# A one-core decoder layer in fp32r halves: gate of the first column split, place of the state update, grouping of the sample's cached values

## The chip, the core and the metric

The kernel runs on one core of one Trainium2 chip. The core has TensorE (PE) for matrix products, VectorE (DVE) and ScalarE (ACT) for elementwise work, GpSimd (POOL) for a smaller share of it, and SyncE (SP), whose queue issues the transfers (DMA). The metric is the time on the device of one launch, in microseconds (us), as the median of several runs. Lower is better.

## The reference

One layer of a hybrid decoder is computed for two groups that share the weights: a prompt of 512 tokens, and 8 samples of 4 new tokens each, which have a past of 2048 positions. All is f32.

```python
x = x + 0.5 * _swiglu(_rmsnorm(x, p['ffn1_norm']), p['ffn1_w_gate'], p['ffn1_w_up'], p['ffn1_w_down'])
h = _rmsnorm(x, p['mix_norm'])
aq, ak, av, mq, mk, mv, mo, mi, mf = _project(h, pos, p['w_in'], p['q_norm'], p['k_norm'])
...
att = _dilated_attn_sample(aq, ak, av, attn_cache[0], attn_cache[1])     # prompt: _dilated_attn_prompt
hm, C, n, m = _mlstm_chunk(mq, mk, mv, ig, lf, C0, n0, m0)               # prompt: _mlstm_prompt
hm = _rmsnorm(hm, p['ml_out_norm']) * jax.nn.sigmoid(mo).reshape(B, T, N_ML_HEADS, ML_DV)
mix = jnp.concatenate([att, hm], axis=-1)
x = x + mix @ p['w_out']
x = x + 0.5 * _swiglu(_rmsnorm(x, p['ffn2_norm']), p['ffn2_w_gate'], p['ffn2_w_up'], p['ffn2_w_down'])
...
C_new = w_c[..., None, None] * C + jnp.einsum('bhs,bshk,bshv->bhkv', w_s, k, v)
n_new = w_c[..., None] * n + jnp.einsum('bhs,bshk->bhk', w_s, k)
```

`D_MODEL` is 1024 and the FFN's width 2816. There are 8 attention heads of 64 and 4 mLSTM heads of 128. A sample's attention reads cached keys and values of the last 2048 positions, at three dilations. The new mLSTM state `C_new`, `n_new` of each sample is an output.

## The kernel before

The 512 + 32 = 544 tokens lie along the free dimension of every activation, split into two halves of 272, and the features lie along the 128 partitions. To keep f32 accuracy, each f32 operand is split into two fp32r numbers, a high half (`xh`, `hh`, `oh`, `mh`, `whi`) and the rest (`xl`, `hl`, `ol`, `ml`, `wlo`), and a product is three matmuls: `whi` with both halves of the activation, and `wlo` with the high one. A weight column block is split by ACT (the cast that makes `whi`) and then DVE (the subtraction that makes `wlo`).

Work on PE is a list of jobs. An ordinary job (class `Job`) is one column of 128 outputs over up to 8 blocks of inputs, 48 matmuls of 272 columns where there are 8. A `Fast` job computes a 2 by 2 block product by a scheme with seven multiplications in place of eight; it has seven steps of 24 matmuls. A step's weight operand is either a raw block or a sum of blocks, made by DVE (`ws`, and at step 4 `wraw<-wraw`), then split. Steps 0, 2, 4 and 6 add into a bank named "a" (tile `mm`), steps 1 and 3 into bank "c" (two tiles `aux`), and step 5 into bank "b"; after steps 0 and 2 among others ACT copies a bank to SBUF (tile `p`). In the traces `oh`, `ol` are halves of activation blocks and of their differences (`xn`, `xd`). A unit is the place of a step or of half an ordinary job: a `Fast` job counts 7 units, an ordinary one 2. Most `Fast` jobs come in pairs, and the first of a pair follows ordinary jobs, which are other columns.

Nothing in the program's order is left to the chip. A planner (class `Order`) keeps a clock for each engine, prices every instruction, and writes the instructions of each engine in the order of the planned times. Pieces of work are generators. A generator yields a time before which it need not go on, a priority, and optionally a condition. `od.spawn(generator, priority)` adds one. `R(tile)` is the planned time at which a tile is ready. On the chip every engine then runs its own list in order, and waits at semaphores.

The places that the change touches:
- `run.splitter` (lines 628 to 639) splits the weights ahead of use, strictly one job after another. For a `Fast` job at unit `pos[n]`, step 0 and the steps from 2 on may be split when PE has come to within 2 units of them, step 1 within 3. An ordinary job may be split 4 units ahead (3 behind a `Fast` job). `whi`, `wlo` and `ws` share a pool of 8 tiles (`wsp`), and the raw weights have three (`wraw`).
- `sample_att` (lines 1471 to 1515) is the attention of the samples over the values, in two groups of four samples. For each of 7 blocks of cached positions, a quad of four tiles `kv` (one a sample, 128 x 512 f32) is loaded by `load_cache`, and four matmuls of 32 rows by 512 columns run side by side (`pTA` holds the weights of blocks 0 to 3, `pTB` the rest). `prefetch` loads a quad; it is called for the next one, and, once the event `("far", 1)` has been set (the scores over the far keys of the second group are done), for the one after it too. It skips what is loaded already. Behind the last quad come `pmk`, small products with `c_sel`, and the columns `attn`, which the `w_out` jobs need as their first operands.
- `ml_head` (lines 1606 to 1753) is one of four mLSTM heads: the prompt's chunks, then the sample outputs, then the norm factors `rs`, which scale `hN` (prompt, by POOL) and `hS` (samples, by DVE). Behind that comes the update of the sample states: per half of the samples (`C0[0]`, `C0[1]`) two products of `vb` and `kws` on PE, four updates on DVE (`C<-C,W,aux`), a copy `nS` on POOL and an output DMA. Then come the transposes of `hN`, the product of `c_own` and `hS`, `hf`, its gate on POOL (on DVE for the last head), and the split into `mh`, `ml`, which `w_out` needs.
- `ml_finish` (line 1755) writes the small outputs `n_p` and `n_s` from `nP` and `nS` after the last head.

Of the kernel before, what the change touches and what calls it, by code (L numbers as in the profile page):

```python
# [16 lines left out]
P = 128  # L17
D = 1024
S = 512
# [33 lines left out]
class Order:  # L53
# [26 lines left out]
    def done(self, *tiles, kind="aux"):  # L80
        for p in tiles:
            self.free[kind].append(self.used[p.tensor.name][0] + 0.2)
# [60 lines left out]
    def R(self, *aps):  # L143
        return max(self.ready.get(a.tensor.name, (0.0, ""))[0] for a in aps) + 0.2
# [103 lines left out]
def hybrid_layer_kernel(ctx: ExitStack, tc: tile.TileContext, I: dict, C: dict, O: list):  # L248
# [20 lines left out]
    def aux():  # L269
        return pax.tile([P, 512], F32, name="aux", tag="aux")  # L270
# [337 lines left out]
    def run(jobs):  # L608
        raws = []
        pos, n = [], 0  # L610
        for j in jobs:
            for r in (j.top, j.low) if isinstance(j, Fast) else (j.raw,):
                if r not in raws:
                    raws.append(r)
            pos.append(n)
            n += 7 if isinstance(j, Fast) else 2

        def loader():
            for n, r in enumerate(raws):
                if n >= 3:  # L620
                    old = raws[n - 3]
                    yield 0, 0, lambda: old.left == 0
                    yield U(old.t)
                if r.t is None:
                    r.load()
            yield 0

        def splitter():
            for n, j in enumerate(jobs):
                if isinstance(j, Fast):  # L630
                    for s in range(7):
                        raw = j.low if s else j.top
                        yield 0, 0, lambda: unit[0] >= pos[n] + s - (3 if s == 1 else 2) and raw.t is not None
                        yield from j.split(s)
                else:
                    ahead = 3 if n and isinstance(jobs[n - 1], Fast) else 4
                    yield 0, 0, lambda: unit[0] >= pos[n] - ahead and j.raw.t is not None
                    yield R(j.raw.t) - 0.3
                    yield from j.split()

        od.spawn(loader(), 0)
        od.spawn(splitter(), 1)
        od.poll()

        def slot():
            od.need(lambda: od.avail("mm", 1))
            od.take("mm", 1)
            ps = pmm.tile([P, 2, 512], F32, name="mm", tag="mm")
            od.poll()
            return ps  # L650

        def products(j, ps, ks, hs=(0, 1)):
            od.need(lambda: j.w is not None)
            hi, lo = j.w
            for k in ks:
                od.need(lambda: j.xs(k) is not None)
                xh, xl = j.xs(k)
                for a, (w, x) in enumerate(((hi, xh), (hi, xl), (lo, xh))):
                    for h in hs:
                        mm(ps[:, h, :HN], w[:, k, :], x[:, h * HN:(h + 1) * HN],  # L660
                           start=j.start and k == 0 and a == 0, stop=j.stop and k == j.nk - 1 and a == 2)
                od.poll()

        def finish(j, ps):
            if j.stop:
                od.spawn(j.after(ps[:, :, :HN], ps), 0)
                od.poll()

        kept = [None]

        def fast(j, more):
            bank = {"a": kept[0] or slot()}
            for n, (name, b) in enumerate(j.steps):
                unit[0] += n > 0
                od.need(lambda: j.w[n] is not None)
                hi, lo = j.w[n]
                if n == 1:
                    od.need(lambda: sum(f <= od.t for f in od.free["aux"]) >= 2)
                    od.take("aux", 2)
                    bank["c"] = aux(), aux()  # L680
                elif n == 5:
                    bank["b"] = slot()
                for i in range(2):
                    ps = bank[b][i] if b == "c" else bank[b][:, i]
                    for k in range(4):
                        od.need(lambda: j.op(name, k) is not None)
                        xh, xl = j.op(name, k)
                        for a, (w, x) in enumerate(((hi, xh), (hi, xl), (lo, xh))):
                            mm(ps[:, :HN], w[:, 4 * i + k, :], x, start=n in (0, 1, 5) and k == 0 and a == 0,
                               stop=k == 3 and a == 2, skip_group_check=True)  # L690
                        od.poll()
                od.spawn(j.post(n, bank, more), 0)
                od.poll()
            kept[0] = bank["b"] if more else None

        first = [(j, slot()) for j in jobs[:2]]
        for ks in (range(0, 4), range(4, 8)):
            for i, (j, ps) in enumerate(first):
                for k in ks:
                    products(j, ps, (k,))  # L700
                    used[0] = max(used[0], k + 1)
                    od.poll()
                if 7 in ks:
                    finish(j, ps)
                    at[0], unit[0] = i + 1, pos[i + 1]
        for i, j in enumerate(jobs[2:]):
            at[0], unit[0] = i + 2, pos[i + 2]
            if isinstance(j, Fast):
                fast(j, isinstance(jobs[i + 3], Fast))
                continue  # L710
            if j.start:
                ps = slot()
            if j is jobs[-1]:
                for h in range(2):
                    products(j, ps, range(j.nk), (h,))
                    od.spawn(last_half(h, ps[:, h, :HN]), 0)
                    od.poll()
                continue
            products(j, ps, range(j.nk))
            finish(j, ps)  # L720
# [748 lines left out]
        out.append((pts[0], pts[1], dn))  # L1469

    def sample_att():
        seq = [(g, i) for g in range(2) for i in range(FAR + 1)]
        vts = {}

        def prefetch(n):
            for g, i in [x for x in seq[n:n + 1] if x not in vts]:
                vts[(g, i)] = [load_cache(vc, 4 * g + b4, i) for b4 in range(4)]

        attn = small("attn", (P, NH // 2, B, T))
        n = 0  # L1480
        for g in range(2):
# [6 lines left out]
            yield R(pa_, pb_)  # L1488
            yield 0, 1
            p = aux()  # L1490
            for i in range(FAR + 1):
                if ("far", 1) in ev:
                    prefetch(n + 1)
                quad = vts.pop((g, i))
                yield R(*quad)
                w = (pa_ if i < 4 else pb_)[:, (i % 4) * P:(i % 4 + 1) * P]
                for b4, v in enumerate(quad):
                    mm(p[32 * b4:32 * b4 + 32, :], w[:, 32 * b4:32 * b4 + 32], v,
                       start=i == 0, stop=False, beside=b4 > 0, tile_position=(0, 32 * b4))
                n += 1  # L1500
                prefetch(n)
            for b4 in range(4):
# [19 lines left out]
            mixed[j] = (xh, xl)  # L1522

    H = [dict() for _ in range(NM)]

    def ml_k(h):
        def post(ps, full):
# [78 lines left out]
    def ml_head(h):  # L1606
# [35 lines left out]
        ss = small("ss", (P, CH + 1), 2)  # L1642
        hN, hS = t2("hN", (P, CH, P)), small("hS", (P, P), 2)

        Cs = [None]
        for c0 in range(0, CH, 2):
            yield 0, 1
# [58 lines left out]
        yield from rsqrt(rs, ss, tt)  # L1706
        pool.tensor_tensor(hN, hN, bc(rs[:, 0:CH], 2, P), op=OP.mult)
        dve.tensor_scalar(hS, hS, rs[:, CH:CH + 1], None, op0=OP.mult)
        pk = []
        for i, c0 in enumerate(C0):  # L1710
            if len(pk) == 2 * i:
                yield R(*C0[i:]) - 0.2, 2
                pk += [aux(), aux()]
                if i == 0 and sum(f <= od.t for f in od.free["aux"]) >= 2:
                    od.take("aux", 2)
                    pk += [aux(), aux()]
                for e in range(2 * i, len(pk)):
                    r_ = slice(NS * e, NS * e + NS)
                    mm(pk[e][:, 0:2 * V1], kws[r_], vb[r_].rearrange("p b v -> p (b v)"), beside=e > 2 * i,
                       tile_position=(r_.start, 0))  # L1720
            for b in range(HB):
                at_ = S + T * (HB * i + b) + T - 1
                o = pk[2 * i + b // 2]
                dve.scalar_tensor_tensor(c0[:, b], c0[:, b], W[:, at_:at_ + 1], o[:, b % 2 * V1:(b % 2 + 1) * V1],
                                         op0=OP.mult, op1=OP.add)
                if b % 2:
                    done(o)
            yield R(c0) - 0.2
            pool.tensor_copy(nS[:, i * HB:(i + 1) * HB, h], c0[:, :, P])
            dma.dma_start(C_s[0, i * HB:(i + 1) * HB, h].rearrange("b k v -> k b v"), c0[:, :, 0:P])  # L1730
        hf = t2("hf")
        yield R(hN, hS), 1
        p = aux()
# [19 lines left out]
            od.spawn(ml_finish(), 3)  # L1753

    def ml_finish():
        yield 0, 1
        pn = aux()
        tr(pn[0:NM, 0:P], nP, ident)
        tr(pn[0:B * NM, P:2 * P], nS.rearrange("p b h -> p (b h)"), ident)
# [189 lines left out]
```

## Time and profile before

| | us |
|---|---|
| median of 3 runs | 1116.19 |
| lowest, highest | 1116.14, 1116.45 |
| profiled execution, its own time | 1116.02 |
| its span | 1114.2 |
| PE busy, DVE busy, ACT busy, POOL busy | 1095.4, 750.6, 507.9, 94.1 |

The mean granted clock of TensorE in the profiled execution was 0.999. The first FFN and the input projection run up to 666 us, then come the `w_out` jobs (their last matmul with `mh` starts at 727.6) and the second FFN. DMA moved 145.36 MB, 130 GB/s in the mean; the values are among them with 56 transfers of 256 KB.

In the rows that follow, a line "start, duration, engine, line, operation, out<-in" is one instruction or, with x and a count, several in a row; the bracket at its end tells how long the engine stood idle before it, and who released it. A row of the view of waits tells the total of such idle time, how often, and the longest.

### The profile page before, as it was taken

To read this page: it belongs to the slowest core of one execution; us is meant where nothing else is said; L and a number is where in the kernel's file an instruction comes from. 1 tells how busy PE (TensorE), PEld (TensorE's weight loads), DVE (VectorE), ACT (ScalarE), POOL (GpSimd) and SP (SyncE) were. 2 spreads that over 40 slices of the span, in tenths; PEclk is the share of its full clock that TensorE was granted. 3 is DMA by queue.
4 is the path that set the end of the run, shared out by engine and by line. 5 is a ranking of instruction groups with operands and counts; after the bars stand their busy time and mean duration, and the time that the engine had idled before them with its cause. 6 is when DMAs were issued, how large, how long until landed. Compare 5 with 4: busy or idle time off the path is not lost.

```text
span 1114.2 us, 21328 instructions
## 1 busy us (share of the span) xinstructions
PE 1095.4 (98%) x8807; PEld 1043.7 (94%) x8807; DVE 750.6 (67%) x1178; ACT 507.9 (46%) x926; POOL 94.1 (8%) x104
## 2 busy tenths in 40 slices
PE   7999999999999999999999999999999999999998
PEld 5999999999999999998887977999999999999997
DVE  5888338873487779678776746688862788537852
ACT  5545215551255455466744544453541355314541
POOL 0000000000000000174444310000000000000000
PEclk9999999999999999999999999999999999999999
DMA  7214412342134547684987494341242222422232
GB/s 234 79 39 132 126 48 77 111 155 76 39 95 132 169 148 168 192 247 125 308 271 252 158 320 155 104 131 56 76 151 76 77 76 76 152 77 76 67 108 58
DMA packets 143404, 145.36 MB, mean 130 GB/s; under 512 B 9028, under 2 KB 120964, under 8 KB 143308
## 3 DMA queue, kind: packets, MB, share of 16 engines
q1 hardware_dynamic: 143244, 144.01, 41.8%
q8 instruction: 69, 1.13, 0.4%
q14 instruction: 27, 0.22, 0.1%
q0 software_dynamic: 64, 0.00, 0.0%
HBM read 132.57 MB, written 9.18 MB: 127 GB/s over the span
## 4 chain that ended last, share of the span: by engine, by line
PE 89%; DVE 6%; ACT 2%; issue 1%; DMA 1%; SPq 0%; DVEq 0%; ACTq 0%
PE mm L288 73%; PE aux L288 13%; PE aux L294 4%; DVE wlo L226 2%; ACT whi L226 2%; DVE ws L226 1%; DVE wraw L226 1%; DMA wraw<-in_ffn_w_up_dram 1%; DMA xt<-in_x_prompt_dram 0%; DVE zu L226 0%; DVE ol L226 0%; ACT p L226 0%; DVE xd L226 0%; SPq L226 0%; DVE hl L226 0%
## 5 line engine op out<-in xcount | busy, mean ns | idle before, releaser
L226 ACT CAST whi<-wraw 128x1024 fp32r<-128x1024 f32 (+3 forms) x180 | 174.2, 988 | 130.5 <-PE mm L288 97.2
L226 DVE TENSOR_TENSOR wlo<-wraw,whi 128x1024 fp32r<-128x1024 f32 (+3 forms) x180 | 208.2, 1165 | 22.8 <-ACT whi L226 22.7
L288 PE MATMUL mm<-oh,wlo 128*128 128x272 f32 x720 | 209.6, 291 | 2.1 <-DVE wlo L226 2.0
L288 PE MATMUL mm<-oh,whi 128*128 128x272 f32 x720 | 207.5, 288 | 0.0
L288 PE MATMUL mm<-ol,whi 128*128 128x272 f32 x720 | 207.2, 288 | 0.0
L288 PE MATMUL mm<-xh,whi 128*128 128x272 f32 x704 | 153.7, 300 | 0.2 <-ACT whi L226 0.2
L288 PE MATMUL mm<-hh,whi 128*128 128x272 f32 x704 | 147.3, 289 | 0.5 <-DVE x L226 0.5
L288 PE MATMUL mm<-xl,whi 128*128 128x272 f32 x704 | 146.0, 289 | 0.5 <-DVE xl L226 0.5
L288 PE MATMUL mm<-hl,whi 128*128 128x272 f32 x704 | 146.5, 288 | 0.0
L288 PE MATMUL mm<-hh,wlo 128*128 128x272 f32 x704 | 146.4, 288 | 0.0
L288 PE MATMUL mm<-xh,wlo 128*128 128x272 f32 x704 | 146.0, 289 | 0.3 <-DVE wlo L226 0.3
L288 PEld LDWEIGHTS mm<-oh,wlo 128*128 128x128 f32 x720 | 135.5, 188 | 5.4 <-DVE wlo L226 4.4
L226 DVE SCALAR_TENSOR_TENSOR x<-mm,x 128x544 f32<-128x544 f32 (+1 forms) x49 | 34.9, 713 | 154.9 <-PE mm L288 154.9
L288 PEld LDWEIGHTS mm<-oh,whi 128*128 128x128 f32 x720 | 135.6, 188 | 0.0
L288 PEld LDWEIGHTS mm<-ol,whi 128*128 128x128 f32 x720 | 135.5, 188 | 0.0
L288 PEld LDWEIGHTS mm<-xh,whi 128*128 128x128 f32 x704 | 109.8, 189 | 12.3 <-issue 11.6
L288 PEld LDWEIGHTS mm<-hh,whi 128*128 128x128 f32 x704 | 110.8, 188 | 0.9 <-DVE x L226 0.7
L288 PEld LDWEIGHTS mm<-xl,whi 128*128 128x128 f32 x704 | 110.7, 189 | 0.8 <-DVE xl L226 0.8
L288 PEld LDWEIGHTS mm<-xh,wlo 128*128 128x128 f32 x704 | 110.8, 189 | 0.6 <-DVE wlo L226 0.6
L288 PEld LDWEIGHTS mm<-hh,wlo 128*128 128x128 f32 x704 | 110.9, 188 | 0.0
L288 PEld LDWEIGHTS mm<-hl,whi 128*128 128x128 f32 x704 | 110.7, 188 | 0.0
L226 ACT CAST whi<-ws 128x1024 fp32r<-128x1024 f32 x54 | 56.7, 1051 | 105.9 <-DVE ws L226 105.9
(328 smaller groups left out, 1755.6 us busy)
## 6 DMA issues: line engine op xcount, KB each, us to landing
wraw<-in_ffn_w_gate_dram SPq DMA_DIRECT2D x40, 512.0 KB
wraw<-in_ffn_w_up_dram SPq DMA_DIRECT2D x36, 512.0 KB
wraw<-in_ffn_w_down_dram SPq DMA_DIRECT2D x16, 1024.0 KB
kv<-in_cache_k_win_dram SPq DMA_DIRECT2D x56, 256.0 KB
kv<-in_cache_v_win_dram SPq DMA_DIRECT2D x56, 256.0 KB
wraw<-in_w_in_dram SPq DMA_DIRECT2D x16, 512.0 KB
wraw<-in_ffn_w_down_dram SPq DMA_DIRECT2D x8, 768.0 KB
wraw<-in_w_in_dram SPq DMA_DIRECT2D x6, 1024.0 KB
```

Source lines behind the costliest of these rows:

```text
L226: r = fn(*args, **kw)
L288: nc.tensor.matmul(out, lhsT, rhs, start=start, stop=stop, **kw)
L294: nc.tensor.transpose(out, in_, idn)
```

## The change

Three things are changed.

First, in `splitter`, step 0 of a `Fast` job that follows an ordinary job may be split 4 units ahead in place of 2. A `Fast` job behind a `Fast` job keeps 2, and the gates of the other steps are the same.

Second, in `ml_head`, the update of the sample states becomes a generator of its own, `state()`, which is spawned with priority 1 at the place where the update stood. The chain to `mh` and `ml` goes on beside it. `ml_finish` waits until all four heads' states are through.

Third, in `sample_att`, values are taken two quads at a time (the seventh stays alone). A pair's eight tiles must all be ready before its first matmul. `prefetch` loads a pair, and is called for the next pair after each pair; the look one further ahead is gone, and so is the test for what is loaded already. `prefetch` is called at the end of the first group and at the head of the second one with the same number, so the second group's first pair is loaded twice (SP issues 8 transfers of 256 KB more).

```diff
         def splitter():
             for n, j in enumerate(jobs):
                 if isinstance(j, Fast):
+                    first = 2 if isinstance(jobs[n - 1], Fast) else 4
                     for s in range(7):
                         raw = j.low if s else j.top
-                        yield 0, 0, lambda: unit[0] >= pos[n] + s - (3 if s == 1 else 2) and raw.t is not None
+                        yield 0, 0, lambda: unit[0] >= pos[n] + s - (first, 3, 2)[min(s, 2)] and raw.t is not None
                         yield from j.split(s)
...
     def sample_att():
-        seq = [(g, i) for g in range(2) for i in range(FAR + 1)]
+        seq = [(g, range(i, min(i + 2, FAR + 1))) for g in range(2) for i in range(0, FAR + 1, 2)]
         vts = {}
 
         def prefetch(n):
-            for g, i in [x for x in seq[n:n + 1] if x not in vts]:
-                vts[(g, i)] = [load_cache(vc, 4 * g + b4, i) for b4 in range(4)]
+            for g, ii in seq[n:n + 1]:
+                for i in ii:
+                    vts[(g, i)] = [load_cache(vc, 4 * g + b4, i) for b4 in range(4)]
...
-            for i in range(FAR + 1):
-                if ("far", 1) in ev:
-                    prefetch(n + 1)
-                quad = vts.pop((g, i))
-                yield R(*quad)
...
+            for _, ii in seq[4 * g:4 * g + 4]:
+                yield R(*[v for i in ii for v in vts[(g, i)]])
+                for i in ii:
...
                 n += 1
                 prefetch(n)
...
     H = [dict() for _ in range(NM)]
+    states = []
...
+        def state():
+            pk = []
+            for i, c0 in enumerate(C0):
...
+                pool.tensor_copy(nS[:, i * HB:(i + 1) * HB, h], c0[:, :, P])
+                dma.dma_start(C_s[0, i * HB:(i + 1) * HB, h].rearrange("b k v -> k b v"), c0[:, :, 0:P])
+            states.append(h)
...
         dve.tensor_scalar(hS, hS, rs[:, CH:CH + 1], None, op0=OP.mult)
-        pk = []
-        for i, c0 in enumerate(C0):
...
+        od.spawn(state(), 1)
         hf = t2("hf")
...
     def ml_finish():
-        yield 0, 1
+        yield 0, 1, lambda: len(states) == NM
```

The planner's lists change at many places. On ACT, the first pair of `Fast` jobs behind other columns near 165 us of the profile changes as follows. The `whi<-ws` are the casts of steps 1, 2 and 3, and `p<-mm` the copy of bank "a" after step 0 and, lower, after step 2:

```order
-L226 CAST whi<-ws 128x1024
-L226 COPY p_1854<-mm 128x544
-L226 CAST whi<-ws 128x1024
-L226 COPY p_1887<-aux 128x272 x2
-L226 CAST whi<-ws 128x1024
+L226 CAST whi<-ws 128x1024 x2
+L226 COPY p_1857<-mm 128x544
+L226 CAST whi<-ws 128x1024
+L226 COPY p_1890<-aux 128x272 x2
 L226 COPY p_1919<-mm 128x544
 L226 CAST whi<-wraw 128x1024 x3
```

The cast of step 2 now stands ahead of the copy after step 0, and the cast of step 3 ahead of the copies of bank "c". Three later pairs change in the same way, and the first pair of each FFN does not: there the copy stays ahead of the cast.

On PE, head 2 of the mLSTM read as follows around its transposes of `hN` and the product of `c_own` and `hS`. The rows with `mh`, `ml` are the first `w_out` job; those with `xh` belong to the input projection:

```order
L288 MATMUL mm<-xh,wlo 128x272 x2
L288 MATMUL aux<-vb,kws 128x258 x2
L288 MATMUL aux<-kv,pTA 32x512 x4
L288 MATMUL aux<-mq,mk 128x128 x4
L288 MATMUL aux<-mq,mk 32x32
L294 MATMUL aux<-ident,hN 128x128 x4
L288 MATMUL mm<-mh,whi 128x272 x2
L288 MATMUL mm<-ml,whi 128x272 x2
L288 MATMUL mm<-mh,wlo 128x272 x2
L288 MATMUL aux<-c_own,hS 128x32
```

Here both pairs of `vb,kws` stand ahead of the transposes (the first one is seven rows higher), and `w_out` begins right behind them. In the changed program the same place on PE reads:

```order
L294 MATMUL aux<-ident,scB 128x128 x3
L294 MATMUL aux<-ident,wn 32x128
L294 MATMUL aux<-ident,scA 128x128 x4
L294 MATMUL aux<-ident,hN 128x128 x4
L288 MATMUL mm<-xh,whi 128x272 x2
L288 MATMUL mm<-xl,whi 128x272 x2
L288 MATMUL mm<-xh,wlo 128x272 x2
L288 MATMUL aux<-c_own,hS 128x32
L288 MATMUL mm<-xh,whi 128x272 x2
L288 MATMUL mm<-xl,whi 128x272 x2
```

The transposes now stand 72 matmuls `mm` ahead of the first `w_out` job, and the second pair of `vb,kws` 13 rows behind `c_own,hS`. In the first group the value quads stood one by one between 3456 and 3648 matmuls `mm` from the program's start, and now stand in pairs at 3522, 3558, 3600 and the last one at 3630. In the second group they stood at 3804, 3828, 3840, 3864, 3876, 3888 and 3912, and now stand in pairs at 3846, 3894, 3948 and the last one at 3990, with `c_sel` at 4002. The first `w_out` job begins at 3864 both times, the second part of `w_out`, whose jobs need the columns `attn`, at 4008.

On SP, the loads of the second group's values stood as follows before (`C_7972` and `C_7973` are the states of head 3):

```order
L226 DMA kv<-in_cache_v_win_dram 128x512 x8
L226 DMA E<-uw_d 128x544
L226 DMA W<-uw_d 128x544
L226 DMA C_7972<-in_state_C_dram 128x4x128
L226 DMA C_7973<-in_state_C_dram 128x4x128
L226 DMA x<-x_d 128x544
L226 DMA kv<-in_cache_v_win_dram 128x1x512 x4
```

In the changed program, where a first load of the same eight tiles has been issued eight rows earlier, the place reads:

```order
L226 DMA out_dram<-C_7376 128x4x128
L226 DMA kv<-in_cache_v_win_dram 128x512 x8
L226 DMA E<-uw_d 128x544
L226 DMA W<-uw_d 128x544
L226 DMA C_8009<-in_state_C_dram 128x4x128
L226 DMA C_8010<-in_state_C_dram 128x4x128
L226 DMA x<-x_d 128x544 x2
L226 DMA wraw<-in_w_out_dram 128x3x256
```

The output of head 2's first half of the state has moved ahead of the value loads, and the next quads (eight tiles at once) are now issued ten rows below these eight tiles.

More of the change, by code (lines that the diff above doesn't have):

```diff
@@ L1490, in sample_att @@
             p = aux()
-            for i in range(FAR + 1):
-                if ("far", 1) in ev:
-                    prefetch(n + 1)
-                quad = vts.pop((g, i))
-                yield R(*quad)
[L1496 to L1499, printed above, removed]
+            for _, ii in seq[4 * g:4 * g + 4]:
+                yield R(*[v for i in ii for v in vts[(g, i)]])
+                for i in ii:
+                    w = (pa_ if i < 4 else pb_)[:, (i % 4) * P:(i % 4 + 1) * P]
+                    for b4, v in enumerate(vts.pop((g, i))):
+                        mm(p[32 * b4:32 * b4 + 32, :], w[:, 32 * b4:32 * b4 + 32], v,
+                           start=i == 0, stop=False, beside=b4 > 0, tile_position=(0, 32 * b4))
                 n += 1
@@ L1643, in ml_head @@
         hN, hS = t2("hN", (P, CH, P)), small("hS", (P, P), 2)
+        def state():
+            pk = []
+            for i, c0 in enumerate(C0):
+                if len(pk) == 2 * i:
+                    yield R(*C0[i:]) - 0.2, 2
+                    pk += [aux(), aux()]
+                    if i == 0 and sum(f <= od.t for f in od.free["aux"]) >= 2:
+                        od.take("aux", 2)
+                        pk += [aux(), aux()]
+                    for e in range(2 * i, len(pk)):
+                        r_ = slice(NS * e, NS * e + NS)
+                        mm(pk[e][:, 0:2 * V1], kws[r_], vb[r_].rearrange("p b v -> p (b v)"), beside=e > 2 * i,
+                           tile_position=(r_.start, 0))
+                for b in range(HB):
+                    at_ = S + T * (HB * i + b) + T - 1
+                    o = pk[2 * i + b // 2]
+                    dve.scalar_tensor_tensor(c0[:, b], c0[:, b], W[:, at_:at_ + 1], o[:, b % 2 * V1:(b % 2 + 1) * V1],
+                                             op0=OP.mult, op1=OP.add)
+                    if b % 2:
+                        done(o)
+                yield R(c0) - 0.2
+                pool.tensor_copy(nS[:, i * HB:(i + 1) * HB, h], c0[:, :, P])
+                dma.dma_start(C_s[0, i * HB:(i + 1) * HB, h].rearrange("b k v -> k b v"), c0[:, :, 0:P])
+            states.append(h)
         Cs = [None]
@@ L1708, in ml_head @@
         dve.tensor_scalar(hS, hS, rs[:, CH:CH + 1], None, op0=OP.mult)
-        pk = []
-        for i, c0 in enumerate(C0):
[L1711 to L1730, printed above, removed]
+        od.spawn(state(), 1)
         hf = t2("hf")
```

## The prediction

> **What bounds the kernel now.** I read the head of the page first, then the chain of waits, then what TensorE waits for between 60 and 1050 us.
>
> ```profile
> span 1114.2 us, 21328 instructions
> PE 1095.4 (98%) x8807; PEld 1043.7 (94%) x8807; DVE 750.6 (67%) x1178; ACT 507.9 (46%) x926; POOL 94.1 (8%) x104
> PE 89%; DVE 6%; ACT 2%; issue 1%; DMA 1%; SPq 0%; DVEq 0%; ACTq 0%
> ```
>
> TensorE (PE) is busy for 98% of the span and carries 89% of the chain. So time can only be won where PE is empty, or where one of its instructions takes longer than it must. The view of waits over the FFNs and the mixer names all the empty places that have a releaser:
>
> ```profile
> PE aux L288 <- DVE wlo L226: 2.3, 6, 1.0
> PE mm L288 <- DVE wlo L226: 2.0, 7, 0.9
> PE mm L288 <- DVE ml L226: 1.3, 1, 1.3
> ```
>
> Thirteen waits are for `wlo`, the low half of a split weight column, and one is for `ml`, the low half of a head's output. No wait is for a value tile `kv`. The printed figure counts an empty pipe only, so I look at one wait closely, beside the row of the chain that shows PE at its pace:
>
> ```profile
> 239.66 60.34 PE mm L288 x480
> ...
> 172.04 0.29 PE L288 MATMUL aux<-ol,whi 128*128 128x272 f32 x1
> 172.59 0.39 PE L288 MATMUL aux<-oh,wlo 128*128 128x272 f32 x1 [0.26 <-DVE wlo L226]
> ...
> 175.58 0.29 PE L288 MATMUL mm<-ol,whi 128*128 128x272 f32 x1
> 176.06 0.39 PE L288 MATMUL mm<-oh,wlo 128*128 128x272 f32 x1 [0.19 <-DVE wlo L226]
> ```
>
> At pace, a matmul starts every 60.34/480 = 0.126 us. Here the starts stand 0.55 and 0.48 apart, so the losses are 0.42 and 0.35 where the view prints 0.26 and 0.19. Each wait costs its printed figure plus 0.16. The thirteen waits cost 4.3 + 13 x 0.16 = 6.4 us. The wait for `ml` costs 1.27 + 0.16 = 1.4.
>
> **Part 1, the first split sooner.** The pair around 160 to 178 us shows what is late. DVE first, then ACT:
>
> ```profile
> 163.75 1.22 DVE L226 TENSOR_TENSOR ws<-ws,wraw 128x1024 f32<-128x1024 f32 x1
> 167.71 1.23 DVE L226 TENSOR_TENSOR wlo<-ws,whi 128x1024 fp32r<-128x1024 f32 x1 [2.73 <-ACT whi L226]
> 168.97 1.23 DVE L226 TENSOR_TENSOR ws<-wraw,ws 128x1024 f32<-128x1024 f32 x1
> 171.31 1.23 DVE L226 TENSOR_TENSOR wlo<-ws,whi 128x1024 fp32r<-128x1024 f32 x1 [1.11 <-ACT whi L226]
> 172.45 1.22 DVE L226 TENSOR_TENSOR wraw<-wraw 128x1024 f32<-128x1024 f32 x1
> 174.78 1.23 DVE L226 TENSOR_TENSOR wlo<-wraw,whi 128x1024 fp32r<-128x1024 f32 x1 [1.11 <-ACT whi L226]
> ```
>
> ```profile
> 166.11 0.62 ACT L226 COPY p<-mm 128x544 f32<-128x544 f32 x1 [4.93 <-PE mm L288]
> 166.62 1.05 ACT L226 CAST whi<-ws 128x1024 fp32r<-128x1024 f32 x1
> 170.23 1.05 ACT L226 CAST whi<-ws 128x1024 fp32r<-128x1024 f32 x1 [0.72 <-DVE ws L226]
> 172.12 0.61 ACT L226 COPY p<-mm 128x544 f32<-128x544 f32 x1 [0.84 <-PE mm L288]
> 173.70 2.95 ACT L226 CAST whi<-wraw 128x1024 fp32r<-128x1024 f32 x3 [0.98 <-DVE wraw L226]
> ```
>
> `ws` of step 2 is ready at 164.97, but its cast stands behind the copy of `p`, which idles 4.93 us for step 0 on PE. Nobody needs that copy so soon. In the changed order the cast stands ahead of it. With the same durations, and about 0.04 between dependent instructions: cast of step 2 at 165.0 to 166.1, its `wlo` to 167.3, `ws` of step 3 to 168.6, cast to 169.7, `wlo` to 170.9. PE wants that one at about 172.2 (172.04 and one interval), so 1.2 us are to spare. Then `wraw` to 172.1, the copy of `p` 172.1 to 172.7 (it needs PE's step 2), cast to 173.7, `wlo` of step 4 to 175.0, wanted at about 175.3 with the first stall gone. Both stalls vanish here, the second with only 0.3 to spare: 0.42 + 0.35 = 0.77 won.
>
> Three other pairs have the same swap in the order (near 307, 880 and 1014 us). One of them, 866 to 886, reads:
>
> ```profile
> PE aux L288 <- DVE wlo L226: 0.2, 1, 0.2
> PE mm L288 <- DVE wlo L226: 0.2, 1, 0.2
> ```
>
> That is 0.4 + 2 x 0.16 = 0.7 each, so four places win 0.77 + 3 x 0.7 = 2.9. The remaining two are the FFNs' first pairs. Windows 69 to 90 and 774 to 796, in that order:
>
> ```profile
> PE mm L288 <- DVE wlo L226: 1.1, 2, 0.9
> PE aux L288 <- DVE wlo L226: 0.4, 1, 0.4
> ...
> PE aux L288 <- DVE wlo L226: 1.0, 1, 1.0
> PE mm L288 <- DVE wlo L226: 0.2, 1, 0.2
> ```
>
> ```profile
> 75.82 1.22 DVE L226 TENSOR_TENSOR wlo<-ws,whi 128x1024 fp32r<-128x1024 f32 x1
> ...
> 786.19 0.61 ACT L226 COPY p<-mm 128x544 f32<-128x544 f32 x1
> ```
>
> At the first, DVE runs without a gap into the `wlo` of step 2, and the changed order takes one `wlo` of 1.22 from ahead of it. So the longest wait (0.9 + 0.16) goes, and the later two shift with PE and stay: 1.0 of 1.9 won. At the second, ACT's copy of `p` stays ahead of the cast in the changed order too, so I take 0.25, the part that DVE gives. Sum of part 1: 2.9 + 1.0 + 0.25 = **4.2**, bounded by 2.9 (only the four) and 6.4 (all thirteen).
>
> **Part 2, the state update beside the chain.** The rows of head 2:
>
> ```profile
> 661.12 1.13 DVE L226 SCALAR_TENSOR_TENSOR C<-C,W,aux 128x129 f32<-128x129 f32 x4 [0.21 <-PE aux L288]
> 663.46 1.13 DVE L226 SCALAR_TENSOR_TENSOR C<-C,W,aux 128x129 f32<-128x129 f32 x4 [1.21 <-PE aux L288]
> 673.85 0.70 DVE L226 TENSOR_TENSOR ml<-hf,mh 128x544 fp32r<-128x544 f32 x1
> 674.61 0.52 PE L288 MATMUL mm<-ml,whi 128*128 128x272 f32 x2 [1.27 <-DVE ml L226]
> ```
>
> The eight updates end at 664.6, and only then come the transposes of `hN`, right before the first `w_out` column. In the changed order 72 ordinary matmuls lie between the two, 9 us of PE, so `ml` is ready long before it is wanted: the whole **1.4** goes. No arithmetic is added or removed. What the updates issue themselves moves along: on POOL `hf` now stands behind the first copy of `nS` only, and waits for four updates (1.13 us) and not eight. On SP the output of the first half of head 2's state now stands ahead of the doubled value loads and of head 3's `E`, `W` and state; SP waits there until those four updates are through. All of this is loaded ahead of use, so I cost it at nothing; if that cover were gone, it would come out of the middle's bound below.
>
> **Part 3, values by pairs of quads.** The arithmetic is the same. Two quads stand together, so PE changes to 32-column tiles fewer times. What one change costs:
>
> ```profile
> 653.24 0.41 PE L288 MATMUL mm<-xh,wlo 128*128 128x272 f32 x2
> 653.58 1.07 PE L288 MATMUL aux<-kv,pTA 128*32 128x512 f32 x8
> ```
>
> The second of two matmuls starts 0.126 after 653.24, so the quad follows it by 0.21 and not 0.126: 0.09 more. The order has 7 fewer such entries and as many exits, 14 x 0.09 = 1.2 if all were alike; other pieces take more of their own, so I take a third, 0.4 (bounds -0.3 to 1.2). The Trainium skill (TensorEngine Tiling (Array Packing), Tiling Modes, Key Properties) has a change of tiling mode drain TensorE; a full drain would space those starts by the matmul's 0.29, and 14 x (0.29 - 0.126) would make 2.3, but the 0.21 here speaks for less.
>
> Against it stand new waits, which the trace of before cannot show: the look two quads ahead is gone, so a pair's eight loads are issued after the pair before, and the second group's last pair now stands just ahead of the second `w_out` column, which wants the attention columns:
>
> ```profile
> 642.00:674.00 32.00, 31.31 (x285) 23.50 (x283) 15.50 (x53) 15.61 (x51) 5.59 (x9) 1.00 0.98 334
> ...
> 682.38 0.75 DVE L226 SCALAR_TENSOR_TENSOR pmk<-aux,sdn,c_hmask 128x512 f32<-128x512 f32 x1 [2.32 <-PE aux L288]
> ...
> 685.20 0.19 DVE L226 TENSOR_TENSOR ml<-attn,mh 128x32 fp32r<-128x32 f32 x1
> ```
>
> Eight tiles of 262 KB are 2.1 MB, 6.3 us at the 334 GB/s of that window. Between the pairs stand 48, 54 and 42 ordinary matmuls (6.0, 6.8, 5.3 us) and small products, so the loads come about when they are wanted. From `pmk` to the columns it takes 3.0 us (682.38 to 685.39), most of it covered, but only six matmuls (0.75) follow the small products. Bounds: 0, since no wait for `kv` is in the list above, and 4, two pairs late by 1 and the columns by 2. I take 0.7, near the lower end.
>
> **Sum.** 4.2 + 1.4 + 0.4 - 0.7 = 5.3. The profiled execution took 1116.02, of it 1114.2 span; 1116.02 - 5.3 = 1110.7. The median of 1116.19 stands 0.17 above that execution, so I say **1110.9**.
>
> **Rivals.**
> - *All waits go:* the first pairs win too (6.4) and nothing new comes: 6.4 + 1.4 + 0.4 = 8.2, 1108.0. For it: DVE is at 67%. Against: the copy at 786.19 keeps its place.
> - *The middle gives back* 3 instead of 0.7: 1113.2. For it: DMA share 0.98 from 642 to 674. Against: nothing waited for `kv`.
> - *The sooner split does nothing:* the gates of steps 2 to 4 are unchanged; were their `wlo` held by something else, parts 2 and 3 alone leave 1.1: 1115.1. Against: 4.93 us of idle on ACT.
> - *Slower, by the values' loads:* the condition that kept a quad from being loaded twice is gone, and the second group's first pair is loaded twice, 2.1 MB in a stretch with the DMA engines at 0.98. All loads behind it come 6.3 later, and each of the three later pairs, without the look ahead, is late by some 2: 12.3 lost, 6.0 won otherwise: 1116.2 + 6.3 = 1122.5. It decides once the new waits exceed 6.0 + 2.2 = 8.2. Against: in the order the doubled loads hold the very slot in which before loaded two quads. The Trainium skill (DMA: Bandwidth & Descriptors, Specifications) gives about 358 GB/s as HBM's limit for a core; by it the window has (358 - 334) x 32 us = 0.8 MB free and the doubled load costs 3.7 and not 6.3; the window ran at 0.98 with 334, below that limit, so the row bears the dearer price.
>
> **How the numbers follow.** Chances: the forecast 0.60 (1109.3 to 1112.2), all waits 0.13, the middle 0.13, no effect of the split 0.08, slower 0.06. The range 1108.2 to 1113.5 takes in the bounds of part 1, most of the middle's, and leaves out the last two. About 0.2% (2.2 us) can be told from no change: below 1114.0 is faster. Faster 0.85, same 0.09, slower 0.06.
>
> **What would show it.** Right: the view of waits keeps some three to five waits for `wlo`, all before 90 and near 790 us; ACT's cast of step 2 starts near 165 in the pair around 170; no wait for `ml`. Wrong: PE waiting for `kv` or for an `ml` of the attention columns around 600 to 700 us, or `wlo` waits unchanged at 172 and 176.

## The result, and the profile after

| | before | after |
|---|---|---|
| median, us (4 runs each) | 1116.32 | 1105.40 |
| lowest, highest | 1116.14, 1119.60 | 1104.67, 1106.51 |
| profiled execution, its span | 1116.02, 1114.2 | 1105.79, 1104.0 |

The ratio is 0.9900, with a 95% interval of 0.9884 to 0.9917. The changed kernel, timed twice more beside before, gave 0.9909 (0.9891 to 0.9928) and 0.9918 (0.9905 to 0.9931). The forecast was 1110.9, in a range of 1108.2 to 1113.5: the direction was right, the gain twice the forecast one, and the time lies below the range.

The head of the page after the change, and PE's waits between 60 and 1050 us (idle time in all, times, longest):

```profile
span 1104.0 us, 21354 instructions
PE 1088.8 (99%) x8807; PEld 1042.7 (94%) x8807; DVE 743.4 (67%) x1175; ACT 509.3 (46%) x929; POOL 89.7 (8%) x104
```

```profile
PE aux L288 <- DVE wlo L226: 1.3, 2, 1.0
PE aux L294 <- DVE rq L226: 0.6, 1, 0.6
PE mm L288 <- DVE wlo L226: 0.4, 2, 0.2
```

Of thirteen waits for `wlo` four are left, the wait for `ml` is gone, and one wait is new, for `rq`. PE's own busy time fell by 6.6 us with the same 8807 matmuls. Idle waits are no part of busy time, so more than waits has changed. Where a late column was, ACT and then DVE read now:

```profile
162.87 1.05 ACT L226 CAST whi<-ws 128x1024 fp32r<-128x1024 f32 x1 [4.97 <-DVE ws L226]
163.93 0.61 ACT L226 COPY p<-mm 128x544 f32<-128x544 f32 x1
```

```profile
163.95 1.22 DVE L226 TENSOR_TENSOR wlo<-ws,whi 128x1024 fp32r<-128x1024 f32 x1 [1.17 <-ACT whi L226]
165.21 1.22 DVE L226 TENSOR_TENSOR ws<-wraw,ws 128x1024 f32<-128x1024 f32 x1
167.55 1.22 DVE L226 TENSOR_TENSOR wlo<-ws,whi 128x1024 fp32r<-128x1024 f32 x1 [1.12 <-ACT whi L226]
```

`ws` of step 2 ended at 162.78 (161.56 + 1.22), and its cast starts 0.1 later, as the walk in the prediction had it.

To place the gain, the 7640 matmuls of 128 x 128 weights by 272 columns are counted in order of their starts: the same number is the same point of the work in every kernel here. The table gives by how much each profiled execution is ahead of before's at these points, part by part, in us. "Start" is up to matmul 300 (59 us in before), "FFN 1" up to 3300, "middle" up to 4800 (447.7 to 742.7 us in before), "FFN 2" the rest, up to the start of the last of them.

| kernel | start | FFN 1 | middle | FFN 2 | sum |
|---|---|---|---|---|---|
| changed | 0.90 | 3.18 | 3.12 | 2.93 | 10.13 |
| changed, second (e8) | 1.00 | 3.01 | 2.80 | 2.89 | 9.70 |
| changed, third (e12) | 0.28 | 2.77 | 2.21 | 2.95 | 8.20 |
| e1 split only | 0.92 | 3.12 | -0.03 | 2.39 | 6.41 |
| e2 state only | 0.40 | -0.23 | 0.72 | 0.24 | 1.12 |
| e3 values only | -1.64 | -0.20 | 0.21 | -0.40 | -2.02 |
| e7 split and state | 0.25 | 2.42 | -0.04 | 2.60 | 5.23 |
| e4 no doubled load | -1.74 | 2.52 | 2.80 | 2.77 | 6.37 |
| e5 first split 3 ahead | 1.48 | -0.78 | 3.16 | 0.49 | 4.35 |
| e6 first split 6 ahead | 0.54 | 1.63 | 2.98 | 2.51 | 7.66 |
| e9 quads apart | 1.86 | 3.29 | 1.46 | 2.43 | 9.05 |
| e10, e11 step 2 sooner | -1.54, 1.09 | 3.76, 4.05 | 3.06, 2.49 | 3.52, 3.51 | 8.81, 11.13 |

No part of the change touches the start. What varies there is told in the last section.

### The profile page after: what moved, and what is told of

The parts are those of the page before. It is cut to its first block, busy times and chain, and to the rows that moved or that the text cites. A ratio compares the mean times of both kernels' runs of the same rounds, so it can differ in the third digit from the quotient of the medians.

```text
span 1104.0 us, 21354 instructions
## 1 busy us (share of the span) xinstructions
PE 1088.8 (99%) x8807; PEld 1042.7 (94%) x8807; DVE 743.4 (67%) x1175; ACT 509.3 (46%) x929; POOL 89.7 (8%) x104
## 4 chain that ended last, share of the span: by engine, by line
PE 91%; DVE 5%; DMA 2%; ACT 1%; issue 1%; SPq 0%; DVEq 0%; ACTq 0%
PE mm L288 73%; PE aux L288 14%; PE aux L294 3%; DVE wlo L226 1%; ACT whi L226 1%; DVE ws L226 1%; DMA wraw<-in_ffn_w_up_dram 1%; DMA kv<-in_cache_k_win_dram 1%; DMA xt<-in_x_prompt_dram 0%; DVE wraw L226 0%; SPq L226 0%; DVE ol L226 0%; DVE rz L226 0%; DVE zu L226 0%; DVE C L226 0%
```

## The experiments

### The three parts alone, and the load left out

e1 is before with the line of `splitter` alone, e2 with `state()` alone, e3 with `sample_att` alone. e4 is the changed kernel with one more test:

```diff
             for g, ii in seq[n:n + 1]:
-                for i in ii:
+                for i in ii if (g, ii[0]) not in vts else ():
```

> The kernel before with the first split's gate alone. Theory A (the forecast's price, a wait costs its printed idle time plus 0.16 us): the nine waits for wlo that go are worth 4.2 us, the median 1112.1. Theory B (read from the trace after: the late matmul is itself followed 0.1 us later than usual, so a wait costs its printed time plus 0.26): the FFNs give 1.1 + 1.0 + 0.9 + 0.3 + 1.1 + 1.0 = 5.4 us, the median 1110.9. Both: only four waits for wlo left between 60 and 1050 us (two at the first pair of each FFN), and the wait for ml of 1.3 us stays. If the first 60 us are 0.9 shorter again, they belong to this part; if not, they vary from run to run.

Measured: median 1109.59, ratio 0.9939 (0.9922 to 0.9955). The two FFNs give 3.12 + 2.39 = 5.5 us: theory B, not A. Four waits for `wlo` are left and the wait for `ml` stays. The gain at the start of 0.92 came back here, but not in e3 and e4, so it belongs to no part. Why a wait costs more than was reckoned is seen in the instruction behind the late one, in before:

```profile
172.81 0.29 PE L288 MATMUL aux<-oh,whi 128*128 128x272 f32 x1
172.94 0.29 PE L288 MATMUL aux<-ol,whi 128*128 128x272 f32 x1
```

The late matmul starts at 172.59, the next one 0.22 behind it in place of 0.126, and only the one after that is back at pace. So 0.10 more is lost behind this wait. With the printed time plus 0.26 for all of them, the nine waits that go make 1.16 at the first pair (0.9 + 0.26), 1.0 at the second, 0.9 at each of three more, and with 0.3 at the second FFN's first pair 5.2 us, near the 5.5 measured.

> The kernel before with the state update as a generator of its own, alone. Theory: the wait for ml goes and nothing else, 1.4 to 1.6 us, the median 1114.8; all thirteen waits for wlo stay. Rival: the whole middle gain of 3.1 us comes from the order that this part opens, the median 1113.2.

Measured: 1114.36, ratio 0.9980 (0.9969 to 0.9991). The middle gives 0.72. The wait for `ml` is gone, as expected, but it is not "nothing else": between 440 and 745 us PE now waits

```profile
PE aux L294 <- DVE rq L226: 0.6, 1, 0.6
PE aux L288 <- DVE aT L226: 0.3, 1, 0.3
```

From start to start the wait for `ml` took 1.56 us; these two take 0.85 and 0.62, so the waits win next to nothing and the 0.72 comes from the rest of the changed order. The median lies near the theory's 1114.8, but the interval (1112.8 to 1115.2) holds the rival's 1113.2 too, and "nothing else" was wrong.

> The kernel before with the values by pairs of quads, alone. Theory: fewer changes to 32-column tiles are worth 1.3 us and not 0.4, less 0.6 of new waits, so the median is 1115.0 to 1115.6 with the wait for ml still there. Rival 1 (forecast): 0.4 won, 0.7 lost, 1116.6. Rival 2: the doubled load costs several us when the state update does not make room, above 1118.

Measured: 1116.24, ratio 0.9997 (0.9985 to 1.0009). The middle gives 0.21. The wait for `ml` is gone here too, since the new order moves the head's chain as well, but PE waits for the attention columns, the place that the prediction had named for this part:

```profile
PE aux L288 <- DVE pmk L226: 0.7, 1, 0.7
PE mm L288 <- DVE mh L226: 0.3, 1, 0.3
```

From start to start these two take 0.93 and 0.67, as much as the wait for `ml` did. The theory was wrong about the `ml`; between its time and rival 1's the interval does not decide, and rival 2 falls.

> The changed kernel with the second load of the second group's first pair left out (the test for what is loaded already is back). Theory: the doubled load is hidden, the median is that of the changed kernel within 0.5 us (1105.0 to 1106.0). Rival: the load delays what comes behind it in a window with the DMA engines nearly full, and the time falls by 1 to 6 us (below 1104.5).

Measured: 1106.70, ratio 0.9910 (0.9891 to 0.9929), as the changed kernel's three. The median itself lies 0.7 above the window that the theory gave; the ratio does not, and the profiled execution lost 1.74 at the start, which no part of the change touches. The middle's 2.80 lies among its 2.21 to 3.12. The doubled load of 2.1 MB is hidden, though the window after the change has the DMA engines at 1.00 (columns as before; the last two are DMA share and GB/s):

```profile
642.00:674.00 32.00, 32.00 (x281) 27.29 (x278) 15.32 (x43) 15.64 (x46) 4.64 (x9) 1.00 1.00 337
```

PE is busy for all of these 32 us. Full DMA engines cost nothing here, since PE waits for nothing that they bring.

### Which part of the sooner split pays

e5 has `else 3` and e6 `else 6` in the line of `first`, in place of `else 4`.

> The changed kernel with the first split 3 units ahead in place of 4. In its lists on ACT the copy of p stands ahead of the cast of step 2 again at the four later pairs, as before the change, though step 0 is split sooner than before. Theory (the swap of cast and copy is what pays): both waits for wlo come back at each of these four pairs, eight more than in the changed kernel, 4 x 1.0 = 4.0 us slower than it. Rival (the sooner start of step 0 is what pays): the waits stay away, and the time is that of the changed kernel within 1 us.

Measured: 1111.58, ratio 0.9964 (0.9953 to 0.9975), 6.2 above the changed kernel's 1105.4. All thirteen waits are back, and ACT reads as in before:

```profile
PE aux L288 <- DVE wlo L226: 2.4, 6, 1.0
PE mm L288 <- DVE wlo L226: 2.1, 7, 0.9
```

```profile
164.63 0.62 ACT L226 COPY p<-mm 128x544 f32<-128x544 f32 x1 [4.93 <-PE mm L288]
165.14 1.05 ACT L226 CAST whi<-ws 128x1024 fp32r<-128x1024 f32 x1
```

```profile
162.28 1.22 DVE L226 TENSOR_TENSOR ws<-ws,wraw 128x1024 f32<-128x1024 f32 x1
```

`ws` of step 2 is ready at 163.50, and its cast starts 1.6 later, behind the copy. Step 0 is split one unit sooner here than in before, and nothing is won by that. It is the swap of the copy and the cast that pays at the four later pairs, which lose 3.9 us where 4.0 was expected, and the FFNs' gain without it is -0.78 and 0.49. The rest of the 6.2 was not expected: the first pairs lose their gain too, 1.5 (at the first FFN's the changed kernel had moved a `wlo` away from ahead of `ws`, and here it is back, as in before), and a new wait for `z` (0.4 printed) takes another 0.7.

> The changed kernel with the first split 6 units ahead in place of 4. Theory: at the FFNs' first pairs DVE is the limit (its other halves stand in the queue), so one more split taken from ahead of them shifts the rest: the two waits left at the first pair of the first FFN (0.3 + 0.2 printed, 1.0 with what follows) go or shrink, the second FFN's 1.0 shrinks by no more than 0.5; 1 us faster than the changed kernel. Rival: raw weights, not DVE, set these places, and nothing moves.

Measured: 1108.20, ratio 0.9935 (0.9913 to 0.9956): slower than the changed kernel (1105.35 in e8, beside it), where 1 us faster was expected; the two intervals overlap, but the trace says the same, with 7.1 behind the start where the changed kernel's three have 7.9 to 9.2. At the first pair the waits grew (69 to 90 us, first e6, then the changed kernel):

```profile
PE aux L288 <- DVE wlo L226: 1.0, 1, 1.0
PE mm L288 <- DVE wlo L226: 0.2, 1, 0.2
```

```profile
PE aux L288 <- DVE wlo L226: 0.3, 1, 0.3
PE mm L288 <- DVE wlo L226: 0.2, 1, 0.2
```

DVE in e6 shows why:

```profile
75.45 1.22 DVE L226 TENSOR_TENSOR ws<-wraw,ws 128x1024 f32<-128x1024 f32 x1
76.60 0.72 DVE L226 TENSOR_TENSOR ol<-xd,oh 128x544 fp32r<-128x544 f32 x1
77.23 0.72 DVE L226 TENSOR_TENSOR xd<-xn,xd 128x544 f32<-128x544 f32 x1
77.87 0.72 DVE L226 TENSOR_TENSOR hl<-zu,hh 128x544 fp32r<-128x544 f32 x1
78.50 1.22 DVE L226 TENSOR_TENSOR wlo<-ws,whi 128x1024 fp32r<-128x1024 f32 x1
```

Three instructions of 0.72 stand between the sum and the split of step 3, where the changed kernel has two. DVE has no gap there, so that part of the theory holds; but what is taken from one step's way is put in the next one's.

### What the pairs of quads give

e7 is before with the first split and the state update, its values one quad at a time. e9 is the changed kernel with

```diff
                 for i in ii:
+                    if i > ii[0]:
+                        yield od.t + 0.6
```

> The kernel before with the first split and the state update, values one quad at a time as before. Theory A (the parts add): 5.4 + 0.7 = 6.1 us from the two parts alone, the time 3.2 above the changed kernel; PE changes to 32-column tiles as often as before. Theory B (the middle's 3.1 comes from the state's place alone once the order falls well): the time within 1 us of the changed kernel.

Measured: 1109.12, ratio 0.9945 (0.9927 to 0.9964); the middle gives -0.04. So theory B falls: without the pairs, nothing of the middle's gain is there. Theory A was near in the time (3.7 above the changed kernel) and not in its parts: the state's 0.7 is not there. The wait for `ml` is gone; PE waits elsewhere in the middle (440 to 740 us):

```profile
PE aux L288 <- DVE aT L226: 0.3, 1, 0.3
PE aux L294 <- DMA kv<-in_cache_k_win_dram: 0.2, 1, 0.2
```

> The changed kernel with a pair's eight tiles loaded and awaited as in the change, but its second quad put 0.6 us later in the planner's time, so that ordinary work stands between the two quads at all six pairs. Theory (standing together is what pays): a quad left and entered anew costs 0.22 us more than one that follows a quad (0.52 and not 0.39 behind its last matmul, 0.21 and not 0.126 ahead of its first), so the middle, 447 to 743 us of before, gains 6 x 0.22 = 1.3 us less than the changed kernel's 3.1 and 2.8: 1.5 to 1.8. Rival (the new places of loads and values pay, not the standing together): the middle's gain stays at 2.8 to 3.1.

Measured: the middle's gain is 1.46, where the changed kernel's three executions have 3.12, 2.80 and 2.21. The timed ratio, 0.9937 (0.9913 to 0.9961), lies on the same side, though its interval overlaps the changed kernel's. No wait is for a value tile and the new wait for `rq` is the same, so the standing together pays 0.75 to 1.7 us, 1.25 against the mean. At two of the six pairs it is small products and not ordinary columns that stand between the quads. In the rows, a lone quad in e9 and then a pair in the changed kernel:

```profile
651.33 0.42 PE L288 MATMUL mm<-xh,wlo 128*128 128x272 f32 x2
651.67 1.07 PE L288 MATMUL aux<-kv,pTA 128*32 128x512 f32 x8
652.67 0.52 PE L288 MATMUL mm<-xh,whi 128*128 128x272 f32 x2
653.03 0.42 PE L288 MATMUL mm<-xl,whi 128*128 128x272 f32 x2
```

```profile
652.47 0.41 PE L288 MATMUL mm<-xh,wlo 128*128 128x272 f32 x2
652.81 1.92 PE L288 MATMUL aux<-kv,pTA 128*32 128x512 f32 x16
654.67 0.77 PE L288 MATMUL aux<-pT,vr 128*64 128x128 f32 x10
```

A quad takes 1.00 to the next start, two together 1.86 and not 2.00. The second entry of 0.09 is saved as well, and behind a quad the two next matmuls take 0.36 and not 0.25. That is 0.14 + 0.09 + 0.11 = 0.34 a pair at most, and 6 x 0.23 to 6 x 0.34 = 1.4 to 2.0 us for six pairs.

All starts in the middle give the same answer. In the table, each interval from one matmul's start to the next is put down to a wait, if the second matmul is in the view of waits; or to the tile shapes, if it lies between two shapes of weights (128 x 128, 128 x 32 and others) or within the 128 x 32 ones; or to the rest. Times are in us.

| kernel | changes of shape | waits | shapes | rest |
|---|---|---|---|---|
| before | 141 | 1.56 | 47.85 | 245.59 |
| changed, its three executions | 129 | 0.84, 0.85, 1.14 | 45.75, 46.01, 46.17 | 245.30, 245.35, 245.48 |
| e7 split and state | 143 | 1.06 | 48.52 | 245.45 |
| e9 quads apart | 141 | 0.84 | 47.79 | 244.91 |

So 1.7 to 2.1 us of the middle's gain lie at the shapes, with twelve changes fewer, and 0.4 to 0.7 in the waits. In e9 the twelve changes are back and their gain is gone. In e7 the waits are 0.5 shorter, and two changes more than in before take 0.7.

### A step further

> The changed kernel again, beside the runs of this call. Theory: of the 10.2 us between the two profiles 0.9 lies in the first 21 us, where no instruction was changed, and varies from run to run by up to 2.6; taken from a landmark behind that (the 300th matmul of 272 columns) to the end the gain is 9.2 to 9.4 again, and the ratio to before is 0.9917. Rival: the gain at the start belongs to the change and comes back in full.

Measured: 1105.35; behind the 300th matmul 8.7, less than expected by half a microsecond, nearly all of it in the middle and FFN 1. The ratio of 0.9909 was within 0.001 of the expected one. The gain at the start came back (1.00), as the rival had it; e4 (-1.74) and e12 (0.28), which have the whole of the change or nearly so, show that it does not belong to it.

e10 and e11 are one kernel, the changed one with `(first, 3, 3)` in place of `(first, 3, 2)`.

> The changed kernel with step 2, too, open 3 units ahead, as step 1 is. In its lists the cast of step 2 moves ahead of hh casts at the second pairs' places; the FFNs' first pairs keep their order. Theory: DVE's and ACT's work, not the gate of step 2, is what the four waits left at the first pairs stand behind, so those stay; at most the small waits near 238 and 349 us go: same as the changed kernel within 0.7 us behind the 300th matmul. Rival: step 2's gate is the next bound, and 1 to 2.5 us go at the two first pairs.

> The kernel with step 2 open 3 units ahead again, now beside the changed kernel on one chip. Theory: 1.1 to 1.6 us faster than the changed kernel behind the 300th matmul (gain over before 10.3 against 9.2 and 8.7), from small waits for z and wlo away from the first pairs; the median 1 us below the changed kernel's, though the first 21 us vary by more than that. Rival: one execution's luck, the gain behind the 300th matmul is 8.7 to 9.3.

> The changed kernel a third time, for comparison on the same chip: gain behind the 300th matmul 8.7 to 9.3, ratio to before 0.991.

Measured: e10 1106.08, ratio 0.9907 (0.9885 to 0.9928); e11 1105.07, ratio 0.9912 (0.9896 to 0.9928); e12 1106.72, 0.9918. The four waits at the first pairs stay, as the theory had it. But "the same within 0.7 us" missed: behind the 300th matmul e10 gains 10.4 and e11 10.0, so the rival of one execution's luck falls. In both traces the two FFNs give 7.3 and 7.6 us, where the changed kernel's three give 6.1, 5.9 and 5.7: some 1.5 us more, in pieces of 0.1 to 0.4 at a dozen places, most of them too short for the view of waits to list. In the medians it cannot be told from the changed kernel. e12 itself missed its expectation: 7.9 behind the 300th matmul, 0.8 less than forecast, 0.6 of it in the middle.

## Why the prediction failed

**What bounds the kernel, right.** The waits it named were the ones that mattered, and what it named as left over is what is left: four waits for `wlo`, all at the FFNs' first pairs.

**Part 1, the mechanism right, the size not: 4.2 forecast, 5.5 measured (e1).** The step that failed is "Each wait costs its printed figure plus 0.16". It counted the gap ahead of the late matmul and left out the 0.10 behind it, though the row stood in the same view. The walk itself held: both stalls vanished at all four places, and e5 shows that the swap is the cause. So 2.9 for these four became 3.9. The first pairs gave 1.19 and 0.31, where 1.0 and 0.25 were forecast.

**Part 2, alone, half right.** The wait for `ml` went in every kernel that has the part. But "the whole 1.4 goes" did not become time: e2 kept 0.72, and e7 nothing: the middle is written anew, with other waits (`rq`, `aT`, a key tile) and more changes of tile shape. What else is in e2's 0.72 stays open.

**Part 3, the step that failed most: 0.4 won.** "I take a third" had no row behind it. Only the entry to a quad was priced, and the exit taken as alike: behind a quad the rows show 0.14 for the leaving and 0.11 for the two next matmuls. e9 gives 1.25 for the standing together, 1.4 to 2.0 follow from the rows, and the changes of shape in the whole middle give 1.7 to 2.1. There are 12 fewer of them, where the prediction counted 14. The 2.3 that it worked out for a full drain and set aside stood nearer than its 0.4; whether it is a drain, no run shows.

**New waits, 0.7: the size right by luck, the place wrong.** Not the values' loads and not the columns: in the changed kernel those waits are nil. What waits is PE for `rq` at 531 us, 0.84 from start to start. e2, with the state update alone, has it too, and e3 and e7 do not, so it hangs on the order. DVE and POOL there, in the changed kernel:

```profile
529.08 1.80 DVE L226 TENSOR_TENSOR rq<-rz,rs 128x544 f32<-128x544 f32 x1
...
534.76 0.72 DVE L226 SCALAR_TENSOR_TENSOR mk<-mm,rb 128x544 f32<-128x544 f32 x1 [1.69 <-PE mm L288]
```

```profile
528.67 1.61 POOL L226 TENSOR_TENSOR pr<-kv,qb 128x512 f32<-128x512 f32 x1 [8.12 <-DMA kv<-in_cache_k_win_dram]
...
533.12 2.52 POOL L226 TENSOR_TENSOR pr<-kv,qb 128x512 f32<-128x512 f32 x2 [2.83 <-DVE cb L226]
```

In before the same DVE instruction takes 0.71 to 0.72, with no POOL instruction beside it. Here it takes 1.80 beside a `pr` that has moved next to it. In the second and third executions the two stand together again, and the wait is there again. The Trainium skill (SBUF — State Buffer, Who interferes with whom) has a DVE instruction with two SBUF inputs contend with a GpSimd instruction that reads SBUF, and calls this an exclusive lock. This trace agrees: the longer instruction is the one with two SBUF inputs, by 1.08, and it ends 0.59 behind the end of `pr`. The other traces bear it out: DVE's TENSOR_TENSOR of 128x544 takes over 0.9 us 49 times in the fourteen of them; each of the 49 starts while a POOL instruction runs and ends 0.58 to 0.59 behind it. With one input in a bank (`mm`), as in the second row of DVE, such an instruction takes 0.7 beside the same `pr`.

**The sum.** 1.3 from part 1 and 1.6 from the middle (2.7 in the mean for 1.1) are missing in the forecast, with 0.4 in the FFNs beyond e1's 5.5: 5.3 becomes 8.6, the mean of 9.2, 8.7 and 7.9 behind the 300th matmul. No wait shows those 0.4: in FFN 2 the changed kernel is 0.5 ahead of e1, evenly over some 2800 matmuls, as one execution's pace differs from another's. The rest up to the medians' 10.9 is the start and the spread of single executions; before has one profile only, so what of it is chance stays open. The range's lower end had only "all waits go", with the same two prices in it, and no term for the scatter of the start.

**The rivals.** *All waits go* fell (four stay), though by luck its time of 1108.0 was the nearest, and *The sooner split does nothing* fell with e1. *The middle gives back* fell: the whole gains 2.2 to 3.1 there, and even the parts alone (e2, e3, e7) lose nothing to speak of. *Slower, by the values' loads* fell with e4: PE did not wait for a value tile, with the doubled load or without it.

## What to carry to other kernels

Price a wait by starts, from the last matmul at pace to the next one at pace, and not by the printed idle time: here 0.2 printed meant 0.46. Price a regrouping in the same way, from the rows ahead of, within and behind a group. Where a planner writes the order, parts that were each priced on the old order do not add: 0.7 and 0.2 alone were 2.2 to 3.1 together, so the whole is to be read from the whole order, and a sum of parts needs a wide range.

## What was not expected of the hardware

The kernel's first matmuls run at little more than half pace, and the moment at which this ends moves between executions. In e3 two matmuls take 0.46 from start to start at 20 us (0.228 each), and 0.24 at 24 us:

```profile
20.33 0.66 PE L288 MATMUL mm<-xh,wlo 128*128 128x272 f32 x2
20.79 0.65 PE L288 MATMUL mm<-xh,whi 128*128 128x272 f32 x2
...
24.43 0.41 PE L288 MATMUL mm<-xl,whi 128*128 128x272 f32 x2
24.67 0.41 PE L288 MATMUL mm<-xh,wlo 128*128 128x272 f32 x2
```

In the changed kernel the full pace is there at 17.3 us. Over the fourteen profiled executions the last matmul at the slow pace starts between 15.7 and 22.8 us, and the 300th matmul between 57.4 and 61.0. These 3.6 us are more than the 2.2 that the prediction called the least that can be told, and how much of the scatter of before's runs, from 1113.2 to 1121.3, comes from there cannot be told from its one profile. The Trainium skill (TensorE: Matmul & The Clock Gate, Part 1: The HAM clock gate) has the clock rise after a busy window that runs free of the kernel's start, so that the moment varies from run to run; the rows agree that the moment varies, by 7 us where the skill has half a microsecond to either side. That the clock is the cause is not shown: the granted clock reads 1.00 from 0 to 20 us in before and in e3, while the matmuls still run at the slow pace.
